# A hybrid encoder layer: the bonus operand made beside the attention, and the finish's memory, banks and order rearranged

## The chip, the cores and the metric

One Trainium2 chip, one core of it. The metric is the device time of one execution in microseconds (us); less is better. The engines are PE (TensorE, matrix products), DVE (VectorE), ACT (ScalarE), POOL (GpSimd) and SP (SyncE, which here only issues DMAs).

## What is computed

One layer over 1024 tokens of width 1024, in float32. The reference, cut to what matters:

```python
f = swiglu(rmsnorm(h, pre1), w_gate, w_up, w_down);  h = h + 0.5 * rmsnorm(f, post1)
z = rmsnorm(h, pre2) @ w_in                      # attention q|k|v, then RWKV r|k|v|decay|rate|gate
y_att  = attention(z[..., :1536])                # 8 heads, rotary, three dilated bands
y_rwkv = rwkv7(z[..., 1536:])                    # 8 heads, a forward and a backward scan
h = h + rmsnorm(concat(y_att, y_rwkv) @ w_out, post2)
f = swiglu(rmsnorm(h, pre3), ...);  h = h + 0.5 * rmsnorm(f, post3)

# inside rwkv7, per direction d: a = sigmoid(a0 + ad @ a2)
k_dir = k * (1 + (a - 1) * k_a)
y     = forward scan + backward scan
y     = (y - mean) * rsqrt(var + eps) * lnx_w + lnx_b        # per head of 64
bonus = sum over head (r * (k_dir[0] + k_dir[1]) * r_k) / 2
y     = (y + bonus * v) * (sigmoid(gd) @ g2)
```

## The kernel before

The parts, in order of the text of `run`: the first FFN (with Strassen-like products, 7 instead of 8); the low-rank parts of decay and rate; the attention's projection; the attention, head by head, with the projection of one RWKV stream of 128 columns beside each of the first seven heads (`project_rwkv`, list `streams`); the first two preparations of the scan, with the projection of the values (streams 8 to 11); the scan; the finish; the output projection with post-norm; the second FFN.

Every product of two float32 operands is made from halves: an operand is split into a high part (fp32r, on ACT) and the rest (on DVE, `split`, lines 186 and 187), and three products are summed.

*Order.* The text says what is done and in which priority. A scheduler puts each engine's instructions in order when the program is compiled: an instruction whose inputs are there by its model goes ahead of earlier-written ones that still wait. On the chip each engine, and each DMA queue, then runs its list strictly in that order. Memory is handed from pool to pool tile by tile: a tile of a new pool waits for the tiles that lay at its place before. Pools grow from the left or (`side="right"`) the right end of the memory; PSUM has eight banks, shared out in the same way.

*Streams.* Stream ct of the RWKV projection is r for 0 to 3, k for 4 to 7, v for 8 to 11 (each two heads). `stream` writes r to `rk_d[ct]`; for k it makes the normalised key and, from the rates of both directions (`self.rates`, loaded by `project_rwkv`), the two directions' keys, kept in `ak_d[d][4 + i]`. The backward direction's are kept in reversed order of time.

*The scan.* 16 chunks of 64 tokens in eight blocks n of two chunks; block n handles tokens 128 n onward in the forward direction and the mirrored ones in the backward direction. `prep` (pools sp, 42,272 bytes a partition, and PSUM pool pp, three banks) loads and scales a block's operands; `solve` is a chain of 62 small DVE operations that inverts its triangles; `merge` finishes the inverses on PE; `chain` carries the state through the two chunks and stores y (line 979). A block's operands live in R0, R1 or B0 in turn, R0 and R1 on the right below sp, B0 on the left. `values` (line 915) loads a chunk's uv and sv from POOL's queue. `project_attended` projects the attention's part of the output between the chains and stores it in `hp_d`.

*The finish.* Four token blocks b of 256 columns in the order 1, 2, 0, 3, each in two units g of four heads: eight units (`finish_unit`). A unit loads y of both directions, k of both, r, v and the gate's input sg, all from SP's queue; POOL adds the directions (lines 1001 and 1004), DVE makes the bonus operand k * r_k * r (line 1006), PE centres y (`yc`, line 1002), sums squares (`var`, 1011), the bonus (1018), turns the rstd (1021) and makes the gate (1032); ACT and DVE do the rest and split the result into x. Blocks 1 and 2 (the first half) need the y of chains 0 to 5 only; blocks 0 and 3 need chain 7. Before, pool xr holds x of both halves, and fin0 the units' tiles with three buffers each; both lie on the right, over what was sp and R0.

*The output projection.* `out_weights` loads and splits the lower half of w_out (W). `out_project` makes, for each of four token tiles of a half, two products of 12 matmuls (`pw`, line 1071), adds them to the tile's row of `hp_d` (line 1102), and calls `done`, which post-norms the row (`post`, lines 256 and 257), stores it, and readies the FFN's input of earlier tiles (`pre`, line 266; `turn`). The first products of the second FFN (factors 1 and 2 of two column blocks) have their weights loaded early into pool wf; the third factor's products are the first that need tiles of the second half.

```python
for half in range(2):
    self.out_project(psum, half, W, x, h2, done)
ready(7)
for j in range(2):
    gate_up.each([(1, j), (2, j)], f, pg)
    turn(6 + j)
```

Of the kernel before, what the change touches and what calls it, by code (L numbers as in the profile page):

```python
# [28 lines left out]
FB = 256  # L29
# [134 lines left out]
class _Kernel:  # L164
# [405 lines left out]
    def stream(self, p, psum, ct, y):  # L570
# [10 lines left out]
        elif ct < 8:  # L581
# [22 lines left out]
            for d in range(2):  # L604
                a = self.rates.pop(0)
# [376 lines left out]
    def finish_unit(self, p, psum, b, g, x, g2w):  # L982
# [13 lines left out]
        y, sq, k, v = z["y0"], z["y1"], z["k0"], z["v"]  # L996
# [7 lines left out]
        G.tensor_tensor(k, k, z["k1"][:, :, ::-1], op=OP.add)  # L1004
        for j in range(2):
            V.scalar_tensor_tensor(k[:, j, :], k[:, j, :], self.rkc[:, 2 * g + j:2 * g + j + 1], z["r"][:, j, :],
                                   op0=OP.mult, op1=OP.mult)

# [3 lines left out]
        rs = p.tile([128, 8], F32, name="f_rs", tag="f_rs", bufs=2)  # L1012
# [29 lines left out]
    def finish_half(self, p, psum, half, x):  # L1042
        g2w = self.load_g2(p)
        for b in self.blocks[2 * half:2 * half + 2]:
            for g in range(2):
                self.finish_unit(p, psum, b, g, x, g2w)

    def out_weights(self, p, k0, gain=None):

        nc, W = self.nc, []  # L1050
        for k in range(4):
            hl = []
            for dh in range(2):
                raw = p.tile([128, 512], F32, name="wor", tag="wor", bufs=2)
                self.load(raw, self.io["w_out"][0][(k0 + k) * 128:(k0 + k + 1) * 128, dh * 512:(dh + 1) * 512])
# [118 lines left out]
    def run(self):  # L1174
# [5 lines left out]
        with self.top as top:  # L1180
# [126 lines left out]
            for n in range(NB):  # L1307
                if n + 1 < NB:
                    self.merge(n + 1, blk[n + 1], sc, pm)
# [137 lines left out]
```

## Time and profile before

| | us |
|---|---|
| median of 3 runs | 2336.88 |
| lowest and highest | 2333.94, 2343.57 |
| the profiled execution's own time | 2333.77 |
| its span, first to last instruction | 2332.0 |
| PE busy, share of the span | 95% |
| DVE, ACT, POOL busy | 76%, 44%, 24% |
| mean granted clock of PE | 0.968 |

All views come from this one execution; times in them are counted from the span's start. Busy shares are of modelled matmuls that overlap, so a PE shown as busy isn't PE at its peak. In rows of the timeline the bracket gives the idle time of the engine just before and what ended it. "x16: 593/598/636" are the least, middle and greatest duration in ns. Rows of groups give the shapes, the count, the busy time, the mean ns of one, and then the idle time before them.

### The profile page before, as it was taken

To read this page: it belongs to the slowest core of one execution; us is meant where nothing else is said; L and a number is where in the kernel's file an instruction comes from. 1 tells how busy PE (TensorE), PEld (TensorE's weight loads), DVE (VectorE), ACT (ScalarE), POOL (GpSimd) and SP (SyncE) were. 2 spreads that over 40 slices of the span, in tenths; PEclk is the share of its full clock that TensorE was granted. 3 is DMA by queue.
4 is the path that set the end of the run, shared out by engine and by line. 5 is a ranking of instruction groups with operands and counts; after the bars stand their busy time and mean duration, and the time that the engine had idled before them with its cause. 6 is when DMAs were issued, how large, how long until landed. Compare 5 with 4: busy or idle time off the path is not lost. (4 is left out here: it accounts for less than half of the span.)

```text
span 2332.0 us, 41360 instructions
## 1 busy us (share of the span) xinstructions
PE 2205.8 (95%) x15556; PEld 1784.2 (77%) x15556; DVE 1763.1 (76%) x2862; ACT 1016.8 (44%) x1910; POOL 565.2 (24%) x682
## 2 busy tenths in 40 slices
PE   6999999999999998999998999988799999999997
PEld 4788888878877676778777777765578888887886
DVE  8899999975676254677668777737899999996565
ACT  4323333354577412667554554445443323235453
POOL 6243444410000010121111111122424453441000
PEclk8999999999999999999998899999899999999999
DMA  5245544486671514555257655368434454547655
GB/s 155 89 165 170 172 145 172 151 273 191 194 233 78 217 58 119 160 173 180 54 148 207 182 147 155 105 196 281 158 122 171 160 181 140 172 158 266 194 190 180
DMA packets 351965, 388.26 MB, mean 166 GB/s; under 512 B 73491, under 2 KB 256659, under 8 KB 351765
## 3 DMA queue, kind: packets, MB, share of 16 engines
q1 hardware_dynamic: 302048, 278.53, 39.3%
q0 software_dynamic: 29360, 94.44, 10.6%
q10 hardware_dynamic: 20356, 12.66, 1.8%
q8 instruction: 122, 2.00, 0.4%
q14 instruction: 79, 0.64, 0.1%
HBM read 260.68 MB, written 124.85 MB: 165 GB/s over the span
## 5 line engine op out<-in xcount | busy, mean ns | idle before, releaser
L186 ACT ACTIVATE wh<-raw 128x512 fp32r<-128x512 f32 (+1 forms) x273 | 167.9, 627 | 264.4 <-PE gu L81 97.5
L187 DVE TENSOR_TENSOR wl<-raw,wh 128x512 fp32r<-128x512 f32 (+1 forms) x273 | 278.5, 1023 | 5.2 <-ACT wh L186 4.3
L81 PE MATMUL gu<-xh,wh 128*128 128x512 f32 x704 | 277.1, 394 | 1.0 <-ACT xh L186 0.8
L81 PE MATMUL gu<-xl,wh 128*128 128x512 f32 x704 | 275.7, 392 | 0.0
L81 PE MATMUL gu<-xh,wl 128*128 128x512 f32 x704 | 275.7, 392 | 0.0
L415 PE MATMUL pd<-gl,gwh 128*128 128x512 f32 x616 | 240.4, 390 | 2.7 <-DVE gl L187 2.7
L415 PE MATMUL pd<-gh,gwh 128*128 128x512 f32 x616 | 239.5, 390 | 0.6 <-DVE row L86 0.6
L415 PE MATMUL pd<-gh,gwl 128*128 128x512 f32 x616 | 239.7, 389 | 0.0
L86 DVE TENSOR_TENSOR row<-gu,row 128x512 f32<-128x512 f32 x308 | 206.8, 684 | 24.6 <-PE gu L81 23.9
L187 DVE TENSOR_TENSOR gwl<-graw,gwh 128x512 fp32r<-128x512 f32 (+1 forms) x176 | 118.1, 674 | 128.7 <-ACT gwh L186 128.3
L116 POOL DMA_DIRECT2D d_hid<-row x154 | 84.7, 551 | 474.0 <-DVE row L114 451.1
L186 ACT ACTIVATE gwh<-graw 128x512 fp32r<-128x512 f32 (+1 forms) x176 | 101.2, 576 | 190.1 <-PE pd L415 157.4
L81 PEld LDWEIGHTS gu<-xh,wh 128*128 128x128 f32 x704 | 133.5, 190 | 30.0 <-ACT xh L186 2.0
L81 PEld LDWEIGHTS gu<-xl,wh 128*128 128x128 f32 x704 | 133.2, 189 | 27.4
L81 PEld LDWEIGHTS gu<-xh,wl 128*128 128x128 f32 x704 | 133.0, 189 | 27.5
L415 PEld LDWEIGHTS pd<-gl,gwh 128*128 128x128 f32 x616 | 115.6, 188 | 28.0 <-DVE gl L187 4.4
L415 PEld LDWEIGHTS pd<-gh,gwh 128*128 128x128 f32 x616 | 115.5, 188 | 25.6 <-DVE row L86 1.0
L415 PEld LDWEIGHTS pd<-gh,gwl 128*128 128x128 f32 x616 | 115.6, 188 | 23.7
L94 ACT ACTIVATE row<-row 128x512 f32<-128x512 f32 x44 | 27.8, 633 | 223.2 <-DVE row L86 215.6
L187 DVE TENSOR_TENSOR gl<-raw,gh 128x512 fp32r<-128x512 f32 x160 | 112.5, 715 | 15.1 <-ACT gh L186 14.9
L145 POOL TENSOR_TENSOR ws<-ws 128x512 f32<-128x512 f32 x88 | 114.3, 1299 | 1.2
L186 ACT ACTIVATE gh<-raw 128x512 fp32r<-128x512 f32 x160 | 98.0, 621 | 33.1 <-DMA raw<-in_ffn_w_down_dram 19.8
(356 smaller groups left out, 5251.5 us busy)
## 6 DMA issues: line engine op xcount, KB each, us to landing
d_hid<-row POOLq DMA_DIRECT2D x154, 256.0 KB, 2.4
graw<-d_hid SPq DMA_DIRECT2D x132, 256.0 KB, 3.1
raw<-in_ffn_w_gate_dram SPq DMA_DIRECT2D x88, 256.0 KB, 3.1
raw<-in_ffn_w_up_dram SPq DMA_DIRECT2D x88, 256.0 KB, 3.3
ws<-in_ffn_w_down_dram SPq DMA_DIRECT2D x88, 256.0 KB, 4.9
d_ws<-ws POOLq DMA_DIRECT2D x88, 256.0 KB, 2.3
raw<-d_ws SPq DMA_DIRECT2D x88, 256.0 KB, 2.7
raw<-in_ffn_w_down_dram SPq DMA_DIRECT2D x66, 256.0 KB, 3.5
```

The costliest lines, as they stand in the source:

```text
L81: self.K.nc.tensor.matmul(ps, a[:, k, :], b[:, k, :], start=(k == 0 and i == 0), stop=(k == 3 and i == 2))
L86: add = lambda o, x: V.tensor_tensor(o, ps, x, op=OP.add)
L94: A.activation(y[:, 0], y[:, 0], AF.Silu)
L116: put = lambda n, y: G.dma_start(self.hid[n - 1, j // 2], y)
L145: G.tensor_tensor(o, a, b, op=OP.subtract)
L186: self.nc.scalar.activation(h, src, AF.Copy)
L187: (eng or self.nc.vector).tensor_tensor(l, src, h, op=OP.subtract)
L415: T.matmul(ps[x], a[:, ts], b, start=(m == 0 and k == 0), stop=(m == NM - 1 and k == 2))
```

## The change

*The bonus operand.* Beside the attention, `project_rwkv` loads also r (tag rr) for each k stream. `stream` adds the two directions' rates on POOL, multiplies r and k on POOL, scales and shifts the sum on ACT by columns that hold r_k already, multiplies on DVE, and stores the product in a new array `fk_d`, from POOL's queue. So r of a pair of heads must be there when its k comes: the streams go 4, 1, 5, 2, 6, 3, 7 instead of 4, 5, 6, 7, 1, 2, 3. The finish loads this one operand in place of k, k and r, and its add and products go.

*The values.* Streams 8 to 11 are written after both first solves, no longer two after each.

*The finish.* The y loads go from POOL's queue, the others stay on SP's. v has two buffers, sg one, loaded once for a token block. The small rs lies in an edge tile that was only padding. xr holds the first half's x alone (16,384 bytes a partition), fin0 takes 25,600; the second half's x goes to a pool on the left. W gets a pool on the right, its raw columns go into the place of the next FFN's factor. PSUM pool pe is opened before pc, so that pc can go and pe stay: `out_project` of the first half takes its two banks from pe and pm.

*The order.* First half of the finish, W, the first half's rows of `hp_d`, second half of the finish, output projection of the first half (without `done`), the FFN's first weights (in fin0's tiles), `done` of the first half's four tiles, output projection of the second half with `done`. A variable `mark` keeps the priority at the last chain and is not used; the `if True:` has no effect.

```diff
@@ project_rwkv
-            for d in range(2) if 4 <= c0 < 8 else ():
-                a = wide.tile([128, S], F32, name="ra", tag="ra")
-                self.load(a, self.lr_d["a"][d][c0 - 4])
+            for tag, src in (("ra", self.lr_d["a"][0][c0 - 4]), ("ra", self.lr_d["a"][1][c0 - 4]),
+                             ("rr", self.rk_d[c0 - 4])) if 4 <= c0 < 8 else ():
+                a = wide.tile([128, S], F32, name=tag, tag=tag)
+                self.load(a, src)
                 self.rates.append(a)
+            if 4 <= c0 < 8:
+                self.rates.append(wide.tile([128, S], F32, name="rs", tag="rr"))
@@ stream
-            for d in range(2):
-                a = self.rates.pop(0)
+            rates, r, both = self.rates[:2], *self.rates[2:]
+            self.rates.clear()
+            G.tensor_tensor(both, rates[0], rates[1][:, ::-1], op=OP.add)
+            G.tensor_tensor(r, r, y, op=OP.mult)
+            A.activation(both, both, AF.Identity, scale=self.khr[:, i:i + 1], bias=self.k1r[:, i:i + 1])
+            V.tensor_tensor(both, both, r, op=OP.mult)
+            self.nc.gpsimd.dma_start(self.fk_d[i], both)
+            for d, a in enumerate(rates):
@@ finish_unit
-        for nm, src, sl in (("y0", self.y_d[0], ts), ("y1", self.y_d[1], back), ("k0", self.ak_d[0][4:], ts),
-                            ("k1", self.ak_d[1][4:], back), ("r", self.rk_d, ts), ("v", self.v_d, ts)):
-            z[nm] = p.tile([128, 2, FB], F32, name="f_" + nm, tag="f_" + nm)
-            self.load(z[nm], src[ps2, :, sl].rearrange("a p t -> p a t"))
-        sg = p.tile([128, FB], F32, name="f_sg", tag="f_sg")
-        self.load(sg, self.sg_d[:, ts])
+        for nm, src, sl in (("y0", self.y_d[0], ts), ("y1", self.y_d[1], back), ("k", self.fk_d, ts), ("v", self.v_d, ts)):
+            z[nm] = p.tile([128, 2, FB], F32, name="f_" + nm, tag="f_" + nm, bufs=2 if nm == "v" else 3)
+            (self.nc.gpsimd if nm[0] == "y" else self.nc.sync).dma_start(z[nm], src[ps2, :, sl].rearrange("a p t -> p a t"))
-        G.tensor_tensor(k, k, z["k1"][:, :, ::-1], op=OP.add)
-        for j in range(2):
-            V.scalar_tensor_tensor(k[:, j, :], k[:, j, :], self.rkc[:, 2 * g + j:2 * g + j + 1], z["r"][:, j, :],
-                                   op0=OP.mult, op1=OP.mult)
-        rs = p.tile([128, 8], F32, name="f_rs", tag="f_rs", bufs=2)
+        rs = self.edge[:, 8 * g + 8:8 * g + 16]
...
@@ run
-            streams, self.rates = [4, 5, 6, 7, 1, 2, 3], []
+            streams, self.rates = [4, 1, 5, 2, 6, 3, 7], []
...
-            for n, ct in ((0, 8), (1, 10)):
+            for n, cts in enumerate(([], [8, 9, 10, 11])):
                 blk[n] = self.prep(n, sp, pp, (R0, R1)[n])
                 blk[n]["inv"] = self.solve(n, sp)
-                self.project_rwkv(zr, pz, x, [(ct, 1), (ct + 1, 1)])
+                self.project_rwkv(zr, pz, x, [(ct, 1) for ct in cts])
...
+            if True:
+                self.finish_half(fi, pf, 0, x)
+                W = self.out_weights(wo, 4, raw=xb[0].tile([128, 8, 512], F32, name="wor", tag="xh0"))
+                f0 = self.operand(*xb)
+                for t in self.order[:4]:
+                    self.load(h2[t], self.hp_d[t * 128:(t + 1) * 128, :])
+            x += self.operand(None, self.pool(st, "xl"), n=4)
+            self.finish_half(fi, pf, 1, x)
+            self.out_project(lambda dh: (pe.tile([128, 512], F32, name="pw", tag="eo"),
+                                         pm.tile([128, 512], F32, name="pw", tag="mg"))[dh], 0, W, x, h2)
...
-            for half in range(2):
-                self.out_project(psum, half, W, x, h2, done)
+            for i in range(4):
+                done(i)
+            self.out_project(lambda dh: psum.tile([128, 512], F32, name="pw", tag="d"), 1, W, x, h2, done)
```

More of the change, by code (lines that the diff above doesn't have):

```diff
@@ L1044, in finish_half, with out_weights @@
         for b in self.blocks[2 * half:2 * half + 2]:
+            sg = p.tile([128, FB], F32, name="f_sg", tag="f_sg", bufs=1)
+            self.load(sg, self.sg_d[:, b * FB:(b + 1) * FB])
             for g in range(2):
-                self.finish_unit(p, psum, b, g, x, g2w)
-    def out_weights(self, p, k0, gain=None):
+                self.finish_unit(p, psum, b, g, x, g2w, sg)
+    def out_weights(self, p, k0, gain=None, raw=None):
         nc, W = self.nc, []
@@ L1091, in project_attended, with out_project @@
             self.nc.scalar.dma_start(self.hp_d[rows, dh * 512:(dh + 1) * 512], o)
-    def out_project(self, psum, half, W, x, h2, done):
+    def out_project(self, bank, half, W, x, h2, done=None):
         xh, xl = x[half]
@@ L1096, in out_project @@
             t, ts = self.order[half * 4 + i], slice(i * 128, (i + 1) * 128)
-            self.load(h2[t], self.hp_d[t * 128:(t + 1) * 128, :])
+            if half:
+                self.load(h2[t], self.hp_d[t * 128:(t + 1) * 128, :])
             for dh in range(2):
-                ps = psum.tile([128, 512], F32, name="pw", tag="d")
+                ps = bank(dh)
                 self.out_products(ps, W, dh, xh, xl, ts)
@@ L1102, in out_project @@
                 self.nc.vector.tensor_tensor(dst, dst, ps, op=OP.add)
-            done(half * 4 + i)
+            if done:
+                done(half * 4 + i)
     def constants(self):
@@ L1180, in run @@
         with self.top as top:
-            self.pool(top, "edge", side="right").tile([128, 120], F32, name="edge")
+            self.edge = self.pool(top, "edge", side="right").tile([128, 120], F32, name="edge")
             self.constants()
@@ L1290, in run @@
             eo = self.pool(s_eo, "eo")
+            pe = self.pool(s_pe, "ps_e", 1, space=PSUM)
             pc = self.pool(s_ps, "ps_c", 1, space=PSUM)
-            pe = self.pool(s_pe, "ps_e", 1, space=PSUM)
             self.sv = {}
```

52 lines of the change are left out of this document (29 added, 23 removed).

## The prediction

> **What bounds the kernel now.** I read the page first, then the busy time by stage (columns: stretch, its length, then busy time and count for PE, PE's weight loads, DVE, ACT, POOL, then granted clock, DMA share, GB/s).
>
> ```profile
> span 2332.0 us, 41360 instructions
> PE 2205.8 (95%) x15556; PEld 1784.2 (77%) x15556; DVE 1763.1 (76%) x2862; ACT 1016.8 (44%) x1910; POOL 565.2 (24%) x682
> ```
>
> ```profile
> 918.00:1190.00 272.00, 259.32 (x2555) 207.17 (x2555) 178.92 (x463) 169.47 (x389) 48.36 (x64) 0.96 0.47 138
> 1190.00:1300.00 110.00, 96.31 (x1110) 79.67 (x1110) 83.77 (x226) 56.81 (x107) 14.69 (x32) 0.82 0.79 208
> 1513.00:1535.00 22.00, 20.52 (x609) 17.50 (x607) 6.93 (x21) 11.19 (x21) 3.56 (x6) 1.00 0.28 83
> 1535.00:1559.00 24.00, 18.94 (x347) 15.56 (x346) 4.78 (x8) 8.35 (x17) 8.78 (x8) 0.86 0.83 262
> 1559.00:1611.00 52.00, 43.30 (x175) 26.47 (x173) 38.33 (x65) 28.63 (x58) 15.12 (x12) 0.93 0.85 283
> 1611.00:1662.00 51.00, 48.29 (x226) 39.02 (x227) 44.14 (x61) 26.47 (x53) 6.42 (x5) 1.00 0.56 194
> 1662.00:1688.00 26.00, 11.54 (x55) 8.67 (x54) 18.67 (x24) 8.92 (x19) 17.72 (x13) 0.73 0.57 182
> ```
>
> PE is the bound, so the change can only win where PE stands still or runs at a lower clock. The stages are: attention (918 to 1190), the first prep/solve and the value projection (to 1300), chain 6 (1513 to 1535), chain 7 with the start of the finish (to 1559), the rest of the finish (to 1611), output projection and post-norm (to 1662), and a tail until the second FFN's products start (1688). PE's idle time in the last five is 1.5 + 5.1 + 8.7 + 2.7 + 14.5 = 32.4 us. This is what the change works on. The timeline says why PE stands still in chain 7:
>
> ```profile
> 1528.01 0.65 ACT L977 COPY yb<-y 128x256 f32<-128x256 f32 x2
> 1534.95 0.65 ACT L977 COPY yb<-y 128x256 f32<-128x256 f32 x2 [2.17 <-PE y L944]
> 1534.98 0.35 SPq L182 DMA_DIRECT2D g2w<-in_rwkv_g_dram  x1
> 1543.34 1.26 POOL L1001 TENSOR_TENSOR f_y<-f_y,f_y 128x512 f32<-128x512 f32 x1 [6.72 <-DMA d_y<-yb]
> 1544.65 2.07 PE L1002 MATMUL yc<-f_y,k_cen 128*128 128x512 f32 x2 [4.49 <-POOL f_y L1001]
> 1546.66 1.86 PE L944 MATMUL st<-uv,bt 128*64 128x64 f32 x29
> ```
>
> A chunk of a chain takes 6.9 us (between the two copies). The finish's first load, g2w, goes out 0.03 us after chain 6's last copy begins: its memory lies under chain 6's block. Then yc, ahead of the chain's st on PE's queue, waits 4.5 us for the sum of the two y loads, and the chain stands from about 1540 to 1546.7. So chain 7 takes 24 us instead of 13.9. And the finish is fed by DMA (the stretch 1535 to 1611):
>
> ```profile
> DMA packets 18793, 20.97 MB, mean 276 GB/s; under 512 B 1272, under 2 KB 16632, under 8 KB 18787
> ...
> f_k<-d_ak SPq DMA_DIRECT2D x16, 256.0 KB, 5.3
> f_r<-d_rk SPq DMA_DIRECT2D x8, 256.0 KB, 5.5
> ```
>
> with DMA shares of 0.83 and 0.85 above: the loads hold it as much as PE.
>
> **The change, part by part.** *Bonus operand.* From the finish go two of the three loads f_k, f_k, f_r of each of eight units, so 16 x 0.262 = 4.2 MB, 15 us at 276 GB/s; the POOL add; and the DVE products:
>
> ```profile
> L1004 POOL TENSOR_TENSOR f_k<-f_k,f_k 128x512 f32<-128x512 f32 x8 | 11.0, 1370 | 14.7 <-DMA f_k<-d_ak 14.7
> L1006 DVE SCALAR_TENSOR_TENSOR f_k<-f_k,rkc,f_r 128x256 f32<-128x256 f32 x16 | 8.2, 542 | 14.4 <-POOL f_k L1004 14.4
> L257 DVE TENSOR_TENSOR row<-row,res 128x1024 f32<-128x1024 f32 x8 | 10.8, 1355 | 0.0
> L586 ACT ACTIVATE ksq<-us,c_rwkv_k_k x4: 1151/1151/1152, 970.2 to 1076.3; 128x1024 f32<-128x1024 f32 x4
> ```
>
> That is 11.0 us of POOL and 8.2 of DVE off the finish. Four times in the attention come two POOL products of 1024 columns (twice the 1.37: 21.9 us in all), one ACT pass (4 x 1.15 = 4.6), one DVE product (4 x 1.36 = 5.4), one load and one store of 0.5 MB. There PE is busy 259.3 of 272 us, DVE would go from 178.9 to 184, ACT from 169 to 174, POOL from 48 to 70. All lie beside PE: I take 0. If that cover is gone, the ACT and DVE passes in line cost 10 us; the new order of the streams could gain at most PE's 12.7 us of idle time.
>
> *Value projection behind both solves.* Priced from these rows:
>
> ```profile
> L514 PE MATMUL zr<-xh,zh x60: 389/392/500, 1186.3 to 1254.9; 128*128 128x512 f32 x60
> L629 SPq DMA_DIRECT2D d_vt<-vts x32: 359/500/1320, 1209.3 to 1271.0; - x32
> 1284.44 1.00 PE L948 MATMUL xu<-sv,lm 64*64 64x64 f32 x13
> 1610.90 5.76 PE pw L1071 x24
> ```
>
> The projection starts at 1186, before the attention has ended and before anything of prep: an instruction whose inputs are there goes ahead of earlier-written ones that wait, whatever the order of the text. So I take 0. The ends: two blocks of 48 matmuls at 0.24 us (24 in 5.76) fall behind the second solve, +23 us, if DVE's solve starves the shifts that set the projection's buffers free; or all 13.7 us of PE's idle time of this stage goes.
>
> *Memory and banks.* Counted from the code, xr and fin0 now take 16,384 + 25,600 = 41,984 bytes a partition; the prep pool that they replace has 42,272. So they no longer touch chain 6's block, and the first half (it needs chains 0 to 5 only) can load from chain 5's store on, some 20 us before 1535. The trace shows that later-written work is pulled forward (zr, and g2w the moment that its memory is free), so no priority is needed for it. W's splits and the h2 rows too lie where earlier chains end.
>
> PE's work for a unit is 1.02 + 1.05 + 1.10 + 0.65 + 1.03 = 4.9 us:
>
> ```profile
> 1560.76 1.02 PE L1002 MATMUL yc<-f_y,k_cen 128*128 128x512 f32 x2
> 1562.60 1.05 PE L1011 MATMUL var<-k_ones,f_y 128*128 128x2 f32 x8 [0.82 <-ACT f_y L1003]
> 1563.51 1.10 PE L1018 MATMUL bonus<-f_k,k_ones 128*128 128x512 f32 x2
> 1565.05 0.65 PE L1021 MATMUL rstd<-ident,f_y 128*128 128x128 f32 x4 [0.43 <-ACT f_y L1015]
> 1565.54 1.03 PE L1032 MATMUL gate<-f_sg,g2w 128*128 128x256 f32 x4
> ```
>
> Four units, 19.4 us, are pushed into chains 6 and 7, whose own idle time is small: the chains end later, at about 1513 + 22 + 13.9 + 19.4 - 4 = 1564 (4 us: the waits within four chunks), but with four units done instead of one. Moved work is no gain for PE; the gain is the idle time that it fills. Of the 32.4 us the 1.5 + 5.1 + 8.7 + 2.7 = 18.0 us ahead of the tail can go: while the second half waits for chain 7's y, the 96 matmuls of the first output projection (23 us) are now there to run, their two banks and h2 rows being free. The clock, 0.86 and 0.93 in two stretches, would give back 0.14 x 18.9 + 0.07 x 43.3 = 5.7 us; I set that against new waits of the same kind as the 4.5 us one. The tail stays: last tile, post-norm, factor sums, first weights.
>
> *DVE is next.* From 1564 to the products it has 38.3 + 44.1 + 18.7 = 101 us, less three units' share (6.2 of the 8.2, and 3 x 3.7 for what else they do, five passes of 0.7 and one of 0.2) = 84 us. At the density of 1611 to 1662 (44.1 of 51) that takes 97 us, so the products start at 1661 at the earliest: the gain ends at 27.
>
> *Queues.* The y loads, 16, go from SP to POOL. Each issue costs it as these do:
>
> ```profile
> L915 POOL DMA_DIRECT2D uv<-d_vt x32: 593/598/636, 1273.3 to 1536.0; - x32
> ```
>
> 16 x 0.6 = 9.6 us against the 11.0 that leave. A y load that waits for chain 5's store holds the uv and sv loads behind it, and chain 7's st waits for those. Ends: 0, and the 4.5 us wait per unit; I take the wait once, inside the 5.7 above. SP gets k, v, sg, W and rows earlier, in a stretch with a DMA share of 0.28. The Trainium skill (SBUF — State Buffer, "Who interferes with whom") holds that a DMA issued from GpSimd can be stalled by a VectorE operation, because GpSimd writes the descriptors through ports that the two share; this speaks against the move, and by it the sum would be an estimated 22 us worse (rival d). The trace so far disagrees: the 32 issues of L915 took 593 to 636 ns over the whole scan, beside all of DVE's solves.
>
> **Sum.** 2333.77 us is the profiled run's time (span 2332.0 and 1.8 around it); less 18 is 2315.8. The median of the runs, 2336.88, is 3.1 higher; between the two I say 2317.
>
> **Rivals.** (a) It doesn't do what it says: the first half isn't pulled forward, or its loads come no earlier. Then only the DMA cut helps, in 1559 to 1611, where PE idles 8.7 us: 2326. For: nothing in the text gives the first half priority. Against: g2w. Chance 0.17.
>
> (b) Slower. PE runs its queue in order, and every unit pulled forward may stop the chain as the first one does now: 6.7 us from 1540 to 1546.7. Eight such stops instead of one cost 7 x 6.7 = 47, less 18 gained: 2334 + 29 = 2363. It decides from the fifth stop more (34 us) on. For: the y loads now follow their store directly. Against: fewer bytes, and three y buffers, so that only the first units find nothing loaded. Chance 0.15; with (c) and less gain it is the whole of the slower side.
>
> (c) The value order costs its 23 us: 2317 + 23 = 2340, the same within what can be told. Chance 0.09. (d) DVE's passes hold up POOL's issues, so that each of the 16 y loads comes a pass later, 1.36 us by L257's row, 22 us in all if no other work covers it: 2339. Chance 0.04, since L915's row shows no such delay. This is the Trainium skill's rule above (SBUF — State Buffer).
>
> (e) The forecast, from 5 to 27 us gained. Chance 0.55.
>
> **How the numbers follow.** A measurement of this kernel can tell about 0.5%, 11.7 us: faster means below 2325, slower above 2349. Of (e) the part over 12 us gained counts as faster: 0.50 of the 0.55; with it goes 0.08 of (a) and of the attention's bounds. Faster 0.58, same 0.27 (the rest of (a) and (e), (c), (d)), slower 0.15. The range leaves out (b) and a little at the low end: 2296 (27 us, and 12 of the attention's idle time) to 2343 ((c), (d) and 3 us). The forecast's own range is 2307 to 2332.
>
> **What would show it.** The first f_y load before 1525 by this profile's clock, in chain 6; DMA share in the finish below 0.8; var, bonus and gate products between the chunks of chains 6 and 7, and pw products ahead of the second half's first yc; start of products (factors 3) 18 us closer to the end of chain 5. Wrong: PE waiting on f_y sums several times (b), the first xu of chain 0 later than 94 us after the attention's end (c), POOL's DMA issues far over 0.6 us (d), or the attention longer than 272 us.

## The result and the profile after

The changed kernel took 2321.48 us, the median of 7 runs (2320.27 to 2334.23), the kernel before 2333.94 in the runs beside it (7 runs, 2332.12 to 2343.57). The ratio is 0.9951, 95% interval 0.9934 to 0.9968: about 11.5 us faster. The profiled execution took 2320.68 us with a span of 2318.9; the span of before was 2332.0, so 13.1 us are to be found between the two traces.

The page of the changed kernel, and its busy time by stage. The columns are as in the prediction: stretch, length, then busy time and count for PE, weight loads, DVE, ACT, POOL, then clock, DMA share, GB/s.

```profile
span 2318.9 us, 41344 instructions
PE 2197.6 (95%) x15556; PEld 1781.0 (77%) x15556; DVE 1768.7 (76%) x2850; ACT 1022.0 (44%) x1914; POOL 591.5 (26%) x705
```

```profile
919.00:1199.00 280.00, 263.06 (x2577) 210.19 (x2578) 197.17 (x473) 175.97 (x400) 69.17 (x76) 0.96 0.50 150
1199.00:1311.00 112.00, 94.60 (x1135) 79.02 (x1135) 81.01 (x216) 56.62 (x102) 16.20 (x32) 0.79 0.79 205
1514.00:1546.00 32.00, 28.32 (x623) 23.68 (x622) 8.80 (x25) 13.01 (x25) 12.97 (x18) 0.84 0.72 230
1546.00:1564.00 18.00, 17.79 (x355) 14.32 (x355) 9.66 (x16) 12.59 (x25) 2.64 (x4) 1.00 0.37 105
1564.00:1617.00 53.00, 50.29 (x237) 36.83 (x236) 37.32 (x59) 31.03 (x65) 14.57 (x16) 1.00 0.76 269
1617.00:1649.00 32.00, 28.30 (x132) 22.48 (x131) 28.80 (x42) 17.47 (x36) 6.04 (x5) 0.95 0.45 152
1649.00:1677.00 28.00, 18.49 (x88) 14.25 (x88) 21.56 (x27) 11.46 (x22) 21.56 (x13) 0.80 0.53 165
```

The stages are attention; first prep, solve and value projection; chain 6; chain 7; finish; the rest of the output projection; tail. From chain 6 to the second FFN's products PE is busy for 143.2 us, against 142.6 before. Its idle time there is 3.7 + 0.2 + 2.7 + 3.7 + 9.5 = 19.8 us against the 32.4 of before. So in this frame the gain is 12.6 us of PE's idle time, as the prediction looked for it; but not at the places that it named. A few starting points in the two profiled executions show where:

| start of | before, us | after, us | difference |
|---|---|---|---|
| last zq product (projection ahead of the attention) | 906.4 | 906.8 | +0.4 |
| last head's output store (attention ends) | 1189.6 | 1198.5 | +8.9 |
| first xu of chain 0 | 1284.4 | 1297.0 | +12.5 |
| chain 5's second y store | 1511.5 | 1514.4 | +2.9 |
| chain 6's second y store | 1535.8 | 1546.4 | +10.5 |
| chain 7's second y store | 1559.5 | 1563.5 | +4.0 |
| split of the fourth finish unit | 1586.8 | 1587.7 | +0.9 |
| split of the eighth finish unit | 1614.8 | 1617.4 | +2.6 |
| first row add of the output projection | 1610.2 | 1578.1 | -32.1 |
| second FFN's products (factor 3) | 1688.2 | 1676.7 | -11.6 |

The finish units come no earlier. What comes earlier is the work behind them: row adds, post-norm, factor sums. And the attention, the first prep and chain 6 lose time, part of which the scan gives back.

Chain 6 takes 32.0 us from store to store, 24.4 before. Three rows of the changed kernel show where part of this goes:

```profile
1525.44 0.59 ACT L906 COPY tt<-pa 128x512 f32<-128x512 f32 x1 [4.66 <-DMA d_y<-yb]
1526.08 1.92 PE L910 MATMUL pa<-X,lm 32*32 32x32 f32 x64 [2.94 <-ACT tt L906]
1526.00:1538.00 12.00, 11.93 (x265) 10.91 (x265) 1.04 (x2) 7.22 (x14) 6.01 (x8) 0.57 0.77 249
```

ScalarE's queue stands until a store of chain 5 has landed, PE stands for ScalarE, and in the 12 us after that the granted clock is 0.57. In the rest of this chain, and in all of chain 6 before, it is 1.00. That is up to 0.43 of 11.9 us of work, an estimated 5.1 us.

The value order and the order of the streams act on the solves, so their rows belong here too: the transposes that close the solves of blocks 0 and 1, before (L883) and after (L892).

```profile
1251.36 1.08 DVE L883 STREAM_TRANSPOSE X<-Ti 128x512 f32<-128x512 f32 x1
1285.09 1.04 DVE L883 STREAM_TRANSPOSE X<-Ti 128x512 f32<-128x512 f32 x1
```

```profile
1260.15 1.07 DVE L892 STREAM_TRANSPOSE X<-Ti 128x512 f32<-128x512 f32 x1
1288.04 1.05 DVE L892 STREAM_TRANSPOSE X<-Ti 128x512 f32<-128x512 f32 x1
```

The first solve ends 8.8 us later, as late as the attention, the second only 3.0, and chain 5 follows the second (+2.9).

### The profile page after: what moved, and what is told of

Read it like the earlier page. It is cut to its first block, busy times and chain, and to the rows that moved or that the text cites. A ratio compares the mean times of both kernels' runs of the same rounds, so it can differ in the third digit from the quotient of the medians.

```text
span 2318.9 us, 41344 instructions
## 1 busy us (share of the span) xinstructions
PE 2197.6 (95%) x15556; PEld 1781.0 (77%) x15556; DVE 1768.7 (76%) x2850; ACT 1022.0 (44%) x1914; POOL 591.5 (26%) x705
## 5 line engine op out<-in xcount | busy, mean ns | idle before, releaser
L187 DVE TENSOR_TENSOR wl<-raw,wh 128x512 fp32r<-128x512 f32 (+1 forms) x273 | 273.3, 1004 | 3.4 <-ACT wh L186 2.5
```

Source lines behind the costliest of these rows:

```text
L187: (eng or self.nc.vector).tensor_tensor(l, src, h, op=OP.subtract)
```

## The experiments

All ratios are to the kernel before, from runs on the same chip beside it (medians 2334.8 to 2336.8 us in the three larger groups and 2335.8 in the last). Profiled executions differ by 5 us before the first edited instruction (last zq product at 901.9 us in run 5, 907.0 in run 9), so the traces are read from landmark to landmark, not by absolute times. Each edit also moves the order in which the scheduler queues other instructions; so the price of a single part holds what this does too.

**1. The order of the streams alone, on the kernel before.**

```diff
-            streams, self.rates = [4, 5, 6, 7, 1, 2, 3], []
+            streams, self.rates = [4, 1, 5, 2, 6, 3, 7], []
```

> The kernel before with only the order of the streams beside the attention changed (4, 1, 5, 2, 6, 3, 7 in place of 4, 5, 6, 7, 1, 2, 3), no bonus products there. Theory A, it is the order that lengthens the attention, since a k stream with its long tail now lies beside the last head: the attention ends 6 to 9 us later than in the kernel before (8.9 in the changed kernel), nearly all of it in head 7. Theory B, the two POOL products, the ACT pass and the DVE product per k stream lengthen it: here the attention ends within 2 us of the kernel before. Either way the scan gives most of a late start back (in the changed kernel 12.5 us at the first xu had become 2.9 at the end of chain 5), so the time is at most 4 us longer than the kernel before.

Measured: 2347.8 us, ratio 1.0043 (1.0026 to 1.0060): 10 us slower, more than either theory allowed. From the first score to the last head's store the attention takes 257.4 us, 257.1 in the kernel before (theory B). But the second solve closes at 1291.28 instead of 1285.09, the third 8 us later than before (its last step starts at 1342.2 instead of 1333.9), and the scan gives nothing back: chain 5 ends 10.2 us later. VectorE's waits between 1190 and 1345, longest groups first (engine, line, releaser: us, times, longest), of this kernel:

```profile
DVE wol L1062 <- ACT woh L1061: 9.7, 5, 6.1
DVE bk L836 <- DMA kd<-d_ak: 5.3, 3, 2.7
DVE ttmp L879 <- DMA X<-d_x: 4.2, 1, 4.2
```

In the kernel before no wait of the prep for d_ak is among the longest. These are the keys that the k streams make. They are not late themselves: the last is stored at 1177.8 and has landed 5.0 us later, and the first load that reads them goes out at 1190.1. What comes late are loads on SP's queue. The first d_ak load of the second prep, with the row ahead of it in this kernel, then in the kernel before:

```profile
1204.85 6.14 SPq L629 DMA_DIRECT2D d_vt<-vts  x4
1211.04 0.54 SPq L182 DMA_DIRECT2D ka<-d_ak  x1
```

```profile
1199.90 0.50 SPq L182 DMA_DIRECT2D ka<-d_ak  x1
```

With the new order of the streams, stores of the value projection (d_vt) stand ahead of the second prep's loads. Its last d_ak load goes out 43.2 us behind the attention's end instead of 32.7. That the whole 10 us come from there isn't shown.

**2. The bonus operand alone, on the kernel before** (with the order of streams that it needs).

```diff
-            streams, self.rates = [4, 5, 6, 7, 1, 2, 3], []
+            streams, self.rates = [4, 1, 5, 2, 6, 3, 7], []
...
+            G.tensor_tensor(both, rates[0], rates[1][:, ::-1], op=OP.add)
+            G.tensor_tensor(r, r, y, op=OP.mult)
...
-        G.tensor_tensor(k, k, z["k1"][:, :, ::-1], op=OP.add)
...
```

> The kernel before with the bonus operand made beside the attention (with the order of streams that it needs) and the finish reading it, and nothing else of the change: y loads on SP, the first output projection behind both halves. Theory A, the gain of the change comes from the order of the end and not from the operand: the time is within 6 us of the kernel before, the attention about 9 us longer, the stretch from chain 7 to the last finish unit 3 to 9 us shorter, since 4.2 MB of loads, 11 us of POOL and 8.2 us of DVE have gone from it. Rival, the lighter finish is the gain: 10 us or more faster than the kernel before, with the attention's loss recovered in the scan.

Measured: 2338.48 us, ratio 1.0002 (0.9989 to 1.0014). The attention takes 263.0 us from the first score to the last store, 5.6 more than in run 1 with the same order of streams: it is the products that lengthen it. From chain 7's end to the second FFN's products it takes 117.5 us instead of 128.7, 1.4 of it up to the eighth unit's split, 9.8 behind that. Against run 1 the operand is worth 0.0041, 9.6 us. The time is the one of theory A, but not for its reason: the loss by the order hides the gain.

**3. The changed kernel with the value projection put back.**

```diff
-            for n, cts in enumerate(([], [8, 9, 10, 11])):
+            for n, cts in enumerate(([8, 9], [10, 11])):
```

> The changed kernel with the value projection put back, two blocks behind each of the first two solves. Theory A, the order of the projection is worth little at the end: the first xu comes 3 to 4 us earlier than in the changed kernel, and the scan, bound by something else behind it, ends chain 5 within 2 us of the changed kernel; the time is within 3 us of it. Rival, the projection behind both solves costs its delay: first xu and the end both 4 us or more earlier. A third case: the new order was worth something, and the time is 3 us or more longer.

Measured: 2337.76 us, ratio 1.0001 (0.9986 to 1.0017): the third case, and by 11.7 us. Theory A falls. The row of the second solve:

```profile
1301.95 1.04 DVE L892 STREAM_TRANSPOSE X<-Ti 128x512 f32<-128x512 f32 x1
```

That is 13.9 us later than in the changed kernel, of which 2.0 had been there at the attention's end. The second prep's last d_ak load goes out 42.2 us behind that end, as late as in run 1, and 28.6 us in the changed kernel. Chain 5 ends 14.5 us later. The first xu comes only 4.8 us later, so it was the wrong mark to look at.

**4. The changed kernel with the early output projection undone.**

```diff
-            self.out_project(lambda dh: (pe.tile(...), pm.tile(...))[dh], 0, W, x, h2)
...
-            for i in range(4):
-                done(i)
-            self.out_project(lambda dh: psum.tile([128, 512], F32, name="pw", tag="d"), 1, W, x, h2, done)
+            for half in range(2):
+                self.out_project(lambda dh: psum.tile([128, 512], F32, name="pw", tag="d"), half, W, x, h2, done)
```

> The changed kernel with one thing undone: the output projection of the first half is written behind the second half's finish units again, on the two banks that the second half's projection uses, and its post-norms with it; its rows are still loaded early. Theory A, the whole gain of the change is this early projection with its row adds (they start 32 us earlier in the changed kernel): the time goes back to the kernel before or above it, 2332 to 2342 us, with the first row add at 1600 us or later of the span. Rival, the gain lies in the lighter finish units and the early loads: the time stays below 2327.

Measured: 2324.84 us, ratio 0.9939 (0.9920 to 0.9958). Nothing is lost: theory A, which I had read off the two traces, falls as well. With the rows loaded, the scheduler pulls the first row add to 1576.1 also from the later place in the text.

**5. The value order alone, on the kernel before.**

```diff
-            for n, ct in ((0, 8), (1, 10)):
+            for n, cts in enumerate(([], [8, 9, 10, 11])):
...
-                self.project_rwkv(zr, pz, x, [(ct, 1), (ct + 1, 1)])
+                self.project_rwkv(zr, pz, x, [(ct, 1) for ct in cts])
```

> The kernel before with only the value projection moved: all four blocks behind the second solve instead of two behind each of the first two. Theory C, the scan is paced by VectorE's solves, and the projection's passes between the first two preps hold up the second solve: with the projection behind both, the second solve ends about 12 us earlier, the ends of the chains follow it, and the time is 8 to 13 us shorter than the kernel before. Rival, the new order only repairs what the new order of the streams spoils (the last k stream's results, which every prep reads, come later there): on the old order of the streams the second solve ends at most 4 us earlier, and the time is within 4 us of the kernel before, or longer.

Measured: 2334.80 us, ratio 1.0000 (0.9984 to 1.0015). The rival holds at the end: the new value order only repairs what the new order of the streams spoils. (The second solve closes 4.0 us earlier, at 1281.12 against 1285.09, of which 2.5 had been there at the attention's end; the third's last step starts at 1334.1, as before.)

**6. Bonus operand, its streams and the value order, with the old end.** Edits of runs 2 and 5 together.

> The kernel before with the bonus operand, its order of streams and the new order of the value projection, and nothing of the rearranged end (no y loads on POOL, no new memory, banks or early projection). Theory C: what carries the change's gain is the value order and the 8 us of products taken from VectorE in the finish; the time is 2322 to 2328 us against 2337 of the kernel before, so the rearranged end is worth at most 6 us. Rival, the gain of the value order is only kept where the end is rearranged: the time is 2331 or more.

Measured: 2322.41 us, ratio 0.9957 (0.9942 to 0.9972). This is the changed kernel without anything of the rearranged end, and it is as fast: 0.9951 less 0.9957 is -0.0006, with the two intervals taken together plus or minus 0.0023, that is -1.4 us, between 6.8 less and 4.0 more. Theory C holds in its bound.

**7. The changed kernel with the first half made urgent.** The variable mark, chain 7's place in the order of scheduling, is set in the changed kernel but not used.

```diff
-            if True:
+            with self.tc.high_priority(self.tc.cur_priority - mark):
                 self.finish_half(fi, pf, 0, x)
```

> The changed kernel with one thing more: the first half's finish units, the weights W and the rows are put ahead of chain 7 in the order of scheduling (their priority is that of chain 7's start). Theory A, this is the step of the forecast that did not happen: with it two or more units are done before chain 7 ends, and the time is 4 to 10 us shorter than that of the changed kernel (2311 to 2317). Rival B, the units are held by their loads and VectorE paces what follows: the units pulled forward stop the chains, chain 7 ends 5 us or more later, and the time is the same within 4 us or longer.

Measured: 2335.52 us, ratio 1.0018 (1.0001 to 1.0036), 0.0067 or 16 us slower than the changed kernel: rival B. Here the forecast's step does happen: the first four units split at 1554.0, 1561.5, 1569.3 and 1574.5, all before chain 7's store at 1576.5. But chain 7 now takes 33.8 us, and little lies beside the way from its store through the y loads to the sums. The timeline of this kernel, columns as before:

```profile
1581.38 0.72 POOL L1001 DMA_DIRECT2D f_y<-d_y  x1 [9.04 <-DMA d_y<-yb]
1585.43 1.29 DVE L1106 TENSOR_TENSOR row<-row,pw 128x512 f32<-128x512 f32 x2 [10.23 <-DMA row<-d_hp]
1591.68 2.07 PE L1008 MATMUL yc<-f_y,k_cen 128*128 128x512 f32 x2 [12.00 <-POOL f_y L1007]
```

PE stands 12.0 us for one sum. In the changed kernel three units of the first half run behind chain 7's store, beside that way. Work was not lacking here: of the first output projection only the first tile's products had run. The next tile's stand behind yc on PE's queue, and their banks came free only with the row adds, which had waited 10.2 us for rows. Whether rows loaded earlier would have covered the way was not tried.

**8. The changed kernel with W loaded later**, and from ScalarE's queue instead of SP's (mark is chain 6's second y store here).

```diff
-                self.load(r, self.io["w_out"][0][(k0 + k) * 128:...])
+                (self.nc.sync if raw is None else nc.scalar).dma_start(r, self.io["w_out"][0][(k0 + k) * 128:...])
...
+                with self.tc.issue_after(mark.ins):
+                    W = self.out_weights(wo, 4, raw=...)
```

> The changed kernel with the 2 MB of W not loaded at chain 5's end but issued on ScalarE's queue behind chain 6's store. Theory A, it is these 2 MB that hold up chain 5's store, the first y loads and chain 6 (32 us in the changed kernel, 24 in the kernel before): chain 6 takes 24 to 27 us, and the time is 3 to 7 us shorter than that of the changed kernel. Rival C, VectorE paces the end and W's splits, 8 times 0.69 us, then move from chain 6 into the paced stretch behind chain 7: chain 6 gets shorter, but the end of the finish comes as late as before, and the time is within 3 us of the changed kernel or longer.

Measured: 2321.91 us, ratio 0.9955 (0.9936 to 0.9974). W's loads and the first y loads of the changed kernel, and the first y loads of this one:

```profile
1513.58 7.71 SPq L182 DMA_DIRECT2D wor<-in_w_out_dram  x8
...
1525.50 2.89 POOL L1001 DMA_DIRECT2D f_y<-d_y  x4 [9.55 <-DMA wor<-in_w_out_dram]
```

```profile
1516.36 2.89 POOL L1001 DMA_DIRECT2D f_y<-d_y  x4 [3.88 <-DMA d_y<-yb]
```

The bracket of the changed kernel names a load of W, but it is the store that counts (in run 4 the same y load goes out before that load of W has landed): POOL goes on 0.5 us after chain 5's second store has landed, here 0.6 us after. That store takes 10.6 us to land in the changed kernel and 4.9 here. So the 2 MB did hold up the y loads, by 5.7 us of wait. But chain 6 still takes 29.8 us (32.0 with W), chains 6 and 7 together 46.1 instead of 49.1, and from chain 7's end to the products it then takes 119.4 us instead of 113.2. The time is that of rival C, its reason only in part: VectorE has 89.6 us of work there instead of 87.4, and the later units come no earlier (the second splits at 1572.8 against 1573.4, the eighth at 1617.3 against 1617.4). The traces show another part: chain 7's two stores take 9.5 and 12.7 us to land here, 8.2 and 10.0 in the changed kernel, and 2.2 and 2.8 in the kernel before. The second half waits for these stores. That the loads issued around them are the cause is likely and not shown, and what it costs was not measured alone.

**9 and 10. What of the lighter finish counts.** Both are on the kernel before: run 9 leaves out the VectorE products of the bonus, run 10 two of the three bonus loads and the POOL adds.

```diff
-        for j in range(2):
-            V.scalar_tensor_tensor(k[:, j, :], k[:, j, :], self.rkc[...], z["r"][:, j, :], ...)
```

> The kernel before without the 16 VectorE products of the bonus in the finish (the sum of the two k's goes into the bonus unmultiplied); all loads, the POOL adds and everything ahead of the finish stay. Theory D, VectorE paces the stretch from chain 7 to the second FFN's products: the 8 to 9 us of passes come off the time with the idle time between them, 7 to 11 us, ratio 0.995 to 0.997. Rival, the finish is fed by DMA: nothing is gained, within 3 us of the kernel before.

```diff
-                            ("k1", self.ak_d[1][4:], back), ("r", self.rk_d, ts), ("v", self.v_d, ts)):
+                            ("v", self.v_d, ts)):
...
-        G.tensor_tensor(k, k, z["k1"][:, :, ::-1], op=OP.add)
...
-                                   self.rkc[...], z["r"][:, j, :], ...)
+                                   self.rkc[...], v[:, j, :], ...)
```

> The kernel before without two of the three bonus loads of each finish unit (f_k of the second direction and f_r, 4.2 MB in all) and without the POOL adds of the two f_k (11 us); the VectorE products stay, with f_v as the second factor. Theory D: the DMA and POOL work is off the path, since VectorE paces: within 3 us of the kernel before, though the DMA share of the stretch after chain 7 falls from 0.86 to under 0.75. Rival, the finish is fed by DMA: 8 to 15 us shorter.

Measured: without the products 2331.03 us, ratio 0.9975 (0.9961 to 0.9989), 5.8 us; without the loads and adds 2326.14 us, ratio 0.9952 (0.9934 to 0.9969), 11.2 us. Theory D, that VectorE alone paces the end, falls: run 9 gains less than its 7 us, run 10 the 8 to 15 us of the rival. The larger part is loads and POOL adds. One row for each kernel, from chain 7's second store to the second FFN's products: before, run 9, run 10, run 6, after.

```profile
1559.50:1688.20 128.70, 102.83 (x453) 74.17 (x452) 101.34 (x148) 63.77 (x128) 39.47 (x29) 0.92 0.68 228
```

```profile
1558.70:1685.00 126.30, 106.49 (x455) 77.98 (x453) 94.80 (x137) 65.69 (x132) 42.99 (x30) 0.88 0.70 232
```

```profile
1557.90:1679.00 121.10, 101.80 (x460) 76.06 (x458) 97.00 (x148) 65.61 (x134) 37.31 (x25) 0.91 0.66 216
```

```profile
1561.20:1678.00 116.80, 100.79 (x459) 75.02 (x457) 94.05 (x138) 65.91 (x134) 36.74 (x25) 0.93 0.67 224
```

```profile
1563.50:1676.70 113.20, 97.28 (x456) 73.66 (x454) 87.38 (x126) 59.67 (x123) 42.44 (x34) 0.94 0.62 210
```

Run 9 takes 6.5 us of work from VectorE, and the stretch gets only 2.4 us shorter: VectorE idles 4.1 us more (31.5 of 126.3, before 27.4 of 128.7), and the first row add comes no earlier (50.3 us behind chain 7's end, 50.7 before). Run 10 takes 4.3 us of work from it and 7.6 us of the length. The stretch of the changed kernel is 3.6 us shorter than run 6's, with 6.7 us less VectorE work in it (W's splits now lie in the chains); but its chain 6 and 7 took 49.1 us, run 6's 48.3. The DMA share did not fall as theory D had said (0.84 in the 52 us behind chain 7).

**11. The changed kernel with its POOL products on VectorE.**

```diff
-            G.tensor_tensor(both, rates[0], rates[1][:, ::-1], op=OP.add)
-            G.tensor_tensor(r, r, y, op=OP.mult)
+            V.tensor_tensor(both, rates[0], rates[1][:, ::-1], op=OP.add)
+            V.tensor_tensor(r, r, y, op=OP.mult)
```

> The changed kernel with its two POOL products of each k stream in the attention moved to VectorE. In the changed kernel VectorE's rb products took 1.17 us each beside POOL's products, 0.68 in the kernel before. Theory E, the two engines slow each other down: without POOL's products the rb passes go back to 0.7 us, VectorE's busy time in the attention does not grow though it gets eight passes of about 1.25 us more (188 us in the changed kernel, here 183 to 190), the attention is 2 to 6 us shorter, and the time 0 to 6 us shorter than the changed kernel's. Rival, the slower rb passes have another cause: VectorE's busy time grows by 10 us, and the attention gets longer.

Measured: 2325.09 us, ratio 0.9947 (0.9928 to 0.9966), no different from the changed kernel. Behind the bonus operand `stream` multiplies rates and key, in four passes (rb) for each k stream. These passes in the attention, before, after and in this run (busy us, mean ns):

```profile
L611 DVE TENSOR_TENSOR rb<-rb,us 128x512 f32<-128x512 f32 x16 | 10.3, 686 | 0.0
```

```profile
L620 DVE TENSOR_TENSOR rb<-rb,us 128x512 f32<-128x512 f32 x16 | 18.5, 1173 | 0.3 <-ACT rb L619 0.2
```

```profile
L620 DVE TENSOR_TENSOR rb<-rb,us 128x512 f32<-128x512 f32 x16 | 10.9, 684 | 0.0
```

The mean of 1173 ns mixes two kinds. In the changed kernel 12 of the 16 passes take 0.68 to 0.69 us, as before. The other four, the first of each k stream, take 2.55 to 2.87. They begin while POOL multiplies r and k, and each ends 0.55 us behind POOL's product. One of the four:

```profile
1040.84 2.40 POOL L610 TENSOR_TENSOR rr<-rr,us 128x1024 f32<-128x1024 f32 x1 [4.32 <-ACT zh L186]
1041.22 2.57 DVE L620 TENSOR_TENSOR rb<-rb,us 128x512 f32<-128x512 f32 x1
```

So theory E holds for the passes, and not as a slower rate: VectorE stands until POOL's product is done. VectorE is busy 185.5 us in the attention of this run, against 188.4 in the changed kernel, though it does the eight added passes itself. But the attention does not get shorter (264.6 us from the first score to the last store, 264.7 in the changed kernel, 257.1 before). The run doesn't tell whether the standing lengthens the attention, since it puts eight passes of 1.22 us in its place; why the products lengthen it stays open.

**12. The row loads early, alone, on the kernel before.** This was to tell why run 10 gains.

```diff
-            self.load(h2[t], self.hp_d[t * 128:(t + 1) * 128, :])
+            if half:
+                self.load(h2[t], self.hp_d[t * 128:(t + 1) * 128, :])
...
+            for t in self.order[:4]:
+                self.load(h2[t], self.hp_d[t * 128:(t + 1) * 128, :])
             self.finish_half(fi, pf, 1, x)
```

> The kernel before with one part of the rearranged end: the four row loads of the first output projection are written ahead of the second half's finish units instead of in the projection; every byte of the bonus, its POOL adds and its VectorE products stay. Without the two bonus loads per unit (the run with the loads left out), the first row load went out 20.8 us behind chain 7's last store instead of 39.6, the first row add 18.5 us earlier, and the time fell by 0.48%. Theory F, that was the place of the row loads on SP's queue: here the first row load goes out less than 15 us behind chain 7, the first row add comes 12 to 25 us earlier than in the kernel before, and the time is 5 to 11 us shorter (0.995 to 0.998). Rival G, it was the 4.2 MB and POOL's adds themselves: the rows come early, but the second half's y, k and r loads come later by as much, and the time stays within 3 us or gets longer.

Measured: 2346.71 us, ratio 1.0043 (1.0020 to 1.0067): rival G. First row loads on SP in the kernel before, in run 10 and here:

```profile
1599.04 4.55 SPq L182 DMA_DIRECT2D row<-d_hp  x6
```

```profile
1578.70 0.75 SPq L182 DMA_DIRECT2D row<-d_hp  x1
```

```profile
1569.98 0.90 SPq L182 DMA_DIRECT2D row<-d_hp  x2
```

The rows do come early here, and the first row add 18.2 us earlier behind chain 7's end (32.5 against 50.7 us), as in run 10 (32.2). But the second half's loads move behind them on SP. POOL's waits for y, in the kernel before and here (us, times, longest), are no longer in all, but one of them is:

```profile
POOL f_y L1001 <- DMA f_y<-d_y: 18.3, 4, 7.2
```

```profile
POOL f_y L1001 <- DMA f_y<-d_y: 19.6, 3, 14.3
```

The fifth unit splits 42.0 us behind chain 7's end instead of 35.1, and what follows it comes later too. So room on the queue and the DMA has to be made first; an early load only takes it from another. Whether the bytes, the entries on SP's queue or the POOL adds make most of run 10's 11.2 us is not separated.

No run beats the changed kernel by more than the intervals: run 4 has the lowest ratio, 0.9939, but its interval reaches to 0.9958.

## Why the prediction was right in size and wrong in its place

The forecast was 2317 us in a range of 2296 to 2343; 2321.5 lies in it, 4.5 us above the forecast and as much below rival (a) with its 2326. By its mechanism the result is rival (a): the first half is not pulled forward, and the lighter finish gains. Run 6, which has only that, comes to 0.9957 x 2336.9 = 2327. So that the number came within 4.5 us of the forecast is in good part luck: the whole of its 18 us was to come from the rearranged end, and that part has no effect that the runs can tell.

In four steps, from the ratios: order of the streams +10.0 us (run 1), bonus operand -9.6 (run 2 less run 1), value order -10.5 (run 6 less run 2), rearranged end -1.4 (after less run 6). The sum is -11.5, what was measured. The second, third and fourth are differences of two ratios, uncertain by some 5 us each.

*What bounds.* That the gain can only be PE's idle time was right: 32.4 us became 19.8. That the 18.0 us ahead of the tail go and the tail stays was not. They became 10.3, and the tail's 14.5 became 9.5. The clock gave nothing back: by the prediction's sum it costs 0.16 x 28.3 + 0.05 x 28.3 = 5.9 us now, against 5.7.

*Its signs.* The first y load, the DMA share behind the chains (0.76) and the first pw products (1563.0, the second half's first yc 1582.8) came as it said. The second FFN's products came 14.4 us closer to chain 5's end, not 18. Of the signs of being wrong, two came as well: a longer attention (280 us) and a late first xu.

*Memory and banks: the step that failed.* "Four units, 19.4 us, are pushed into chains 6 and 7" with the end of the chains at 1564. The chains do end at 1564, but with one unit done (in the kernel before none, not one: its first split comes 5.8 us behind chain 7's store). That 1564 comes out is luck: chain 6 took 32.0 us and chain 7 17.1, where the working had 22 for chain 6, 13.9 for chain 7 and 19.4 for four units. The first y load goes out early, at 1515.21, as the prediction asked (before 1525); but the next wait 9.55 us, and then two k loads hold SP until 1548:

```profile
1528.27 19.69 SPq L1001 DMA_DIRECT2D f_k<-d_fk  x2
```

The inference from g2w, a load that went out the moment its memory was free, did not carry over to units whose products need a chain of queues, buffers and the place that the scheduler gave them. And had the step come true, it would have been a loss: in run 7 four units are done, and the time is 16 us longer. The step took PE's idle time for time that any moved work can fill, and left out the way from chain 7's store to the second half's sums, which some work has to lie beside. The prediction had rival (b) for that, units that stop the chain, but put its price on the stops alone.

*Bonus operand.* The finish gains about what the bytes and passes say: 11.2 us without the loads and adds and 5.8 without the products, 17.0 in all if the two add up, which no run shows, against 15 us of DMA, 11.0 of POOL and 8.2 of VectorE in the working; 9.6 of it is left once the products are paid for. The attention at 0 was the mis-sized term: the products cost it 5.6 us (run 2 against run 1), and in the changed kernel it is 7.6 us longer, inside the bound of 10. The reason given, that all of it lies beside PE, was not enough.

The rb passes are a second thing that the price of the new products missed: four of the 16 wait for POOL, 7.8 us of VectorE's time in all. The Trainium skill (SBUF — State Buffer, "Who interferes with whom") says that a VectorE instruction with two SBUF inputs contends with a GpSimd instruction that reads SBUF. The traces agree: four passes that begin beside POOL's product end 0.55 us behind it, and with that product gone all 16 take 0.68 us (run 11). I had cited this section for the y loads only.

*Value order at 0.* Right on the kernel before (run 5: 1.0000), wrong in the changed one: 11.7 us (run 3), within its end of 13.7. What was missed is the order of the streams, which had no price of its own in the sum: it costs 10 us (run 1), and the value order gives that back. The part of it that the traces show is SP's queue, where stores of the values stand ahead of the second prep's loads; that this is all of it isn't shown. The mark that the prediction set for it, the first xu at most 94 us behind the attention's end, was missed by 4.5 us (98.5). The kernel before is itself at 94.9, so the mark left no room. And it told of the streams: it is 101.8 with their order alone (run 1), 101.2 with the old value order in the changed kernel (run 3), and 95.9 with the new value order alone (run 5).

*Queues.* POOL's issues of the y loads took 727 ns in the finish, not 600: 11.6 us for 16 instead of 9.6.

```profile
L1001 POOL DMA_DIRECT2D f_y<-d_y x16 | 11.6, 727 | 28.3 <-DMA wor<-in_w_out_dram 9.6 <-ACT yb L986 8.5 <-DVE xl L187 6.6
```

Its longest waits are for a landing store (the row names a load of W that landed then, see run 8), a copy and a buffer. A late y load by a pass each, rival (d), isn't seen: the 16 issues took 722 to 738 ns. Nor was it what the Trainium skill's section named there (SBUF — State Buffer, "Who interferes with whom") gives: it says that tensor_tensor passes were not seen to stall a DMA, and L257's row, from which the 22 us were worked out, is one. The loads were not tried on SP again. Rivals (b) and (c) did not occur in the changed kernel: PE idles 0.2 us in chain 7, its 3.7 us in chain 6 are not for a sum of y, and the value order gains.

*DVE is next.* That the gain ends where VectorE's work does was a bound and was not reached: 87.4 us of it in 113.2 behind chain 7.

## What to carry to other kernels

Idle time of the bound engine tells how much there is to gain, not that moved work will fill it: ask which wait makes the idle time, and what can run beside that wait once the work has gone (run 7). Taking bytes, queue entries and passes away from the last stage paid; moving a load forward on a full queue (run 12) cost as much as the whole order of streams did. A change of many parts is best taken apart in both directions, each part alone and each part undone: here two parts cancel (streams and value order), and the rearranged end, the largest part of the diff, has no effect that the runs can tell. And a mean over a group can hide that a few passes wait and the rest do not (run 11): look at the least and the greatest.

## What the runs showed of the hardware that was not expected

Four VectorE products of two SBUF operands, begun while POOL multiplied 128x1024 elements from SBUF in 2.40 us, took 2.55 to 2.87 us instead of 0.68 and ended 0.55 us behind POOL's. Moving POOL's products to VectorE left VectorE less busy in all (185.5 us against 188.4).

Eight loads of W, 2 MB issued in 7.7 us, lengthened the landing of chain 5's second store from 4.9 to 10.6 us, and with it the wait of POOL's next y loads from 3.88 to 9.55 us. ScalarE stood 4.66 us for a store of the same chain, PE 2.94 us for ScalarE, and in the 12 us after that the granted clock was 0.57.
